# Two late tables of modulation weights loaded earlier, and a different schedule of modulation work in the second layer

## The chip, the cores and the metric

The kernel runs on one core of one Trainium2 chip. The metric is the device time of one execution in microseconds (us); the times given are those of several executions, and one more execution was taken with the hardware profiler. TensorE (PE, with its weight loads PEld) does the matmuls, VectorE (DVE), ScalarE (ACT) and GpSimd (POOL) the rest, and SyncE's queue (SP) issues nearly all transfers.

## What is computed

Two layers of a streaming encoder over 256 positions of width 2048, all in float32. Per layer:

```python
mod = (c_act @ w_mod[l] + b_mod[l]).reshape(bn, 6, d)     # c_act: one vector of 2048
shift_m, scale_m, gate_m, shift_f, scale_f, gate_f = ...  # six vectors of 2048
h = layer_norm(x) * (1.0 + scale_m) + shift_m
proj = h @ w_in[l]
uv, q_c, kv_c, k_r, sb, sc, sh, ag = jnp.split(proj, IN_SPLITS, axis=-1)
y_a = gmlp_mixer(uv, ...)            # u * (W_s LN(v) + b): groups U and V of the kernel
y_b = mla_mixer(q_c, kv_c, k_r, ...) # attention: group B
y_c = short_conv_mixer(sb, sc, sh, ...)   # groups E (sb) and C (sc, sh)
y_d = conformer_conv(ag, ...)        # a * sigmoid(g), a convolution over 31 positions: group D
y = jnp.concatenate([y_a, y_b, y_c, y_d], axis=-1) @ w_out[l]
x = layer_norm(ALPHA * x + (1.0 + gate_m) * y, post_mix_g[l], post_mix_b[l])
h = layer_norm(x) * (1.0 + scale_f) + shift_f
y = conv_ffn(h, ffn_w_up[l], ...)    # up to 2 x 5632 columns, gate convolution, down
x = layer_norm(ALPHA * x + (1.0 + gate_f) * y, post_ffn_g[l], post_ffn_b[l])
```

The six modulation vectors of a layer come from a product of one vector with a 2048 x 12288 matrix, 100 MB per layer. The kernel does this product on VectorE, while TensorE does the large products.

## The kernel before

**Large products.** Weights come in tiles of 1 MB (`raw_tile`, a ring of four buffers of 128 x 2048, which modulation weights, normalisation gains and a few others share). `weights` (L405 to L447) issues the load, lets ScalarE round each half tile to a `whi` (L442) and VectorE form the rest `wlo` (L443); each of these has a ring of four half tiles. The activations are split in the same way into the pairs `hT` (L459, L460), and TensorE adds up hi x hi, hi x lo and lo x hi (`mm`, L83). Some groups use the weights unsplit (`wexact`), with plain float32 matmuls. With `spare`, the first halves of a group go into buffers of another pool, the slots (eleven buffers of 128 x 1024, `thi` and `tlo`), which also hold the activations of the mixers and of the FFN.

**Order.** A group's units are run by `stream`: load a unit, then carry out what is pending (`flush`: the products of the unit before, the evacuation of a finished group), put this unit's products on the pending list, and then let `pump` take some modulation steps. The program text is then ordered by a scheduler that places instructions on each engine as their inputs come; on an engine they run strictly in that order.

**Modulation.** `mod_stream` is a generator that walks through the vectors in a fixed order. One step loads 1 MB of `w_mod` (L338) and multiplies and adds it on VectorE into `macc` (L246, the first of a vector L244). `RATES` says how many steps `pump` takes for each unit of a stage (`phase` sets the stage). `need` makes up for what is missing when a vector is used. A gate vector gets its bias in L345, is split (`mhi`, `mlo`) and spread over the partitions by TensorE into `ps_gate` (`gate_rows`). Layer 1's mixer gate is needed when the first 1024 columns of the output projection are done: there `done` calls `gate_of`, and `finish` (L675 to L679) scales and adds the columns.

**Layer 0's late columns.** Of layer 0's FFN shift and scale, only the first 1536 columns are ready when the FFN begins. The last 512 of each (`LATE_KT`) are computed during the first FFN units: eight loads of 1 MB (L315), four rows blocks of 128 each, with four VectorE instructions each. `first_group` multiplies the first gate columns with the three quarters of the input that are there, its `rest` follows with the last quarter after the units of two other groups.

**Start of a layer's products.** `first_group` (L510) loads its weights, normalises and transposes the input (`to_hT`: `xn` on ScalarE, `ps_xT` on TensorE, `hF` on ScalarE for the first 128 positions and on VectorE, L585, for the others), multiplies, and splits the input for the groups that follow. In layer 1 the first group is U, and `mix_u` (L851, a Gelu on ScalarE) evacuates it in the program's text before the next group, D, loads its weights. In layer 1's FFN `gated_first` (L1260) stands in the same way ahead of the next group's load.

Of the kernel before, what the change touches and what calls it, by code (L numbers as in the profile page):

```python
# [13 lines left out]
P = 128  # L14
D = 2048
# [10 lines left out]
C_UV, C_Q, C_SB, C_SC, C_AG = 0, 1024, 1728, 2240, 3264  # L26
# [5 lines left out]
SHIFT_M, SCALE_M, GATE_M, SHIFT_F, SCALE_F, GATE_F = range(6)  # L32
# [1 line left out]

RATES = [
    dict(B=1.3, C=1.6, out=2.1, first=1.2, up=0.68, down=0.83),
    dict(D=0.2, U=0.4, V=0, B=0.2, C=0.5, E=0.6, out=0.6, up=0.3, down=0.7),
]

STEPS = [  # L40
# [10 lines left out]
LATE_KT = 12  # L51
# [3 lines left out]
def encoder_kernel(ctx: ExitStack, tc: tile.TileContext, A: dict, consts: bass.AP, out: bass.AP):  # L55
    nc = tc.nc
# [13 lines left out]
    def raw_tile(name):  # L70
        return rawp.tile([P, 2048], F32, tag="raw", name=name)
# [16 lines left out]
    def slot(name, dtype=F32):  # L88
        return slotp.tile([P, 1024], dtype, tag="slot", name=name)
# [151 lines left out]
    def mod_step(acc, w, kt, first):  # L241
        col = cact[:, kt : kt + 1]
        if first:
            i = dve.tensor_scalar(out=acc, in0=w, scalar1=col, scalar2=None, op0=ALU.mult)  # L244
        else:
            i = dve.scalar_tensor_tensor(out=acc, in0=w, scalar=col, in1=acc, op0=ALU.mult, op1=ALU.add)  # L246
        held(i, "mod")
# [47 lines left out]
    def settle(i=0):  # L295
        l, m, acc, k0, k1 = late.pop(i)
        if m in (GATE_M, GATE_F):
            gate_rows(l, m, acc)
        elif (l, m) in ((1, SHIFT_F), (1, SCALE_F)):
            mod_rows(l, m, acc)  # L300
        else:
            mod_cols(l, m, k0, acc[:, k0 * P : k1 * P])

    def mod_stream(order):

        held_back = {}
        for l, m in order:
            if (l, m) == (0, GATE_F):  # L310

                for u in range(4):
                    for v, acc in held_back.items():
                        raw = raw_tile("wmod").rearrange("p (k c) -> p k c", k=4)
                        nc.sync.dma_start(  # L315
                            out=raw,
                            in_=A["w_mod"][0, 4 * u * P : 4 * (u + 1) * P, v * D + LATE_KT * P : (v + 1) * D].rearrange(
                                "(k p) c -> p k c", p=P
                            ),
                        )  # L320
                        for k in range(4):
                            mod_step(acc[:, LATE_KT * P :], raw[:, k, :], 4 * u + k, u + k == 0)
                        if u == 3:
                            late.append((0, v, acc, LATE_KT, KT))
                        yield
            while len(late) >= 2:
                if late[0][:2] in WITH_NORM:
                    yield
                else:
                    settle()  # L330
            acc = tmpp.tile([P, D], F32, tag="macc", name="macc", bufs=2)
            k1 = KT
            if l == 0 and m in (SHIFT_F, SCALE_F):
                held_back[m], k1 = acc, LATE_KT
            w = k1 * P
            for kt in range(KT):
                raw = raw_tile("wmod")
                nc.sync.dma_start(out=raw[:, :w], in_=A["w_mod"][l, kt * P : (kt + 1) * P, m * D : m * D + w])  # L338
                if kt == KT - 1 and m in (GATE_M, GATE_F):
                    row = raw_tile("brow")  # L340
                    nc.sync.dma_start(out=row[0:1, :], in_=A["b_mod"][l : l + 1, m * D : (m + 1) * D])
                mod_step(acc[:, :w], raw[:, :w], kt, kt == 0)
                if kt == KT - 1:
                    if m in (GATE_M, GATE_F):
                        dve.tensor_tensor(out=acc[0:1, :], in0=acc[0:1, :], in1=row[0:1, :], op=ALU.add)  # L345
                    late.append((l, m, acc, 0, k1))
                yield
                if kt == 1 and late and late[0][:2] not in WITH_NORM:
                    settle()

    mods = mod_stream(
        [(0, GATE_M), (0, SHIFT_F), (0, SCALE_F), (0, GATE_F), (1, SHIFT_F), (1, SCALE_F)]
        + [(1, SHIFT_M), (1, SCALE_M), (1, GATE_M), (1, GATE_F)]
# [3 lines left out]
    def phase(l, name):  # L357
        pace["rate"] = RATES[l][name]
# [16 lines left out]
    pending = []  # L375
# [22 lines left out]
    def held(i, kind):  # L398

        name, n = hold[kind]  # L400
        if n > 0:
            hold[kind][1] = n - 1
            tc.add_manual_dep(i.ins, name, order_dep, reason="the norm is what the next products wait for")
# [366 lines left out]
    def mixers(l, w_in, Y, hF=None, between=None):  # L770
# [77 lines left out]
        def mix_u(cps, _):  # L848
            Y["a"] = slot("ya").rearrange("p (j s) -> p j s", j=4)
            for b in range(2):  # L850
                act.activation(  # L851
                    out=Y["a"][:, 2 * b : 2 * b + 2, :],
                    in_=cps[b].rearrange("p (j s) -> p j s", j=2),
                    func=AF.Gelu_apprx_tanh,
                )
# [259 lines left out]
        if hF is not None:  # L1115
            return by_pieces(l, w_in, hF, between, mix_d, mix_u, mix_v, mix_b, mix_c, mix_e)
        phase(l, "U")
        mix_u(first_group(w_in, C_UV, f"U{l}", l, SHIFT_M, SCALE_M)[0], None)
        phase(l, "D")
        run(group(w_in, C_AG, 1024, f"D{l}", mix_d, spare=1))  # L1120
        phase(l, "V")
# [115 lines left out]
    def ffn_up(l, G):  # L1237
# [19 lines left out]
        def gated_first(cps, j0=0):  # L1257
            G.append(slot("g").rearrange("p (j s) -> p j s", j=4))
            for b in range(2):
                act.copy(G[j0 // 4][:, 2 * b : 2 * b + 2, :], cps[b].rearrange("p (j s) -> p j s", j=2))  # L1260
            for j in range(4):
                background.append(lambda j=j0 + j: gate_conv(j))

        cps, rest = first_group(w, 0, f"g{l}0", l, SHIFT_F, SCALE_F, LATE_KT // 4 if l == 0 else 4)
        if l == 0:

            gv = group(w, D_FF, 512, "v00", valued_pairs, nk=4, spare=1)
            gg = group(w, 512, 512, "g01", lambda cps, _: gated_first(cps, 4), nk=4)
            phase(l, "first")

            def late():
                needs(l, SHIFT_F, SCALE_F)()
                rest()
                gated_first(cps)

            for g, u in ((gv, 0), (gg, 0), (gv, 1), (gg, 1), (gv, 2), (gg, 2)):
                stream(lambda: g[1](u), lambda item, g=g, u=u: g[2](item, u))
            pending.append(late)
            phase(l, "up")
            for g, u in ((gv, 3), (gg, 3)):  # L1280
                stream(lambda: g[1](u), lambda item, g=g, u=u: g[2](item, u), STEPS[l]["up"])
            pending.extend([gv[3], gg[3]])
        else:
            gated_first(cps)

        for c0 in range(0, D_FF, 512):
            gi, j0 = c0 // 512, c0 // P
# [86 lines left out]
    def needs(l, *ms, k1=KT):  # L1374
        def before():
            for m in ms:
                need(l, m, k1)

        return before
# [114 lines left out]
```

## Time and profile before

| What | us |
|---|---|
| timed executions | 2326.01, 2333.79, 2332.75 (median 2332.75) |
| profiled execution | 2328.31 |
| its span, first to last instruction | 2326.5 |
| TensorE busy | 2255.9 |
| VectorE busy | 1792.9 |
| ScalarE busy | 1011.3 |
| mean granted TensorE clock | 0.986 |

Times within the span, from the timeline of TensorE: layer 0's FFN begins at 437, layer 1's U at 1218, its D at 1254, its output projection at 1467, its FFN at 1570. "Busy" is the sum of instruction times; matmuls are pipelined. The granted clock is the share of full speed that TensorE was allowed in a stretch.

### The profile page before, as it was taken

What the parts mean: (1) busy time and instruction counts of PE and PEld (TensorE: products, weight loads), DVE (VectorE), ACT (ScalarE), POOL (GpSimd) and SP (SyncE); (2) the same over time, 40 slices, a digit from 0 to 9 for tenths busy, and PEclk for the clock granted to TensorE, in tenths of its full rate; (3) what the DMA queues carried; (4) which work ended last, traced back from release to release, by engine and by line L of the source; (5) the groups of instructions that cost most, each with busy time, mean ns of one, the idle gap of its engine ahead of it and who ended that gap; (6) DMA issues with size and microseconds to landing.
All of it is one profiled execution on the core that took longest, in us unless ns stands there. A gap on an engine that the chain in (4) does not pass through costs nothing. (4 is left out here: it accounts for less than half of the span.)

```text
span 2326.5 us, 31205 instructions
## 1 busy us (share of the span) xinstructions
PE 2255.9 (97%) x12331; PEld 1936.7 (83%) x12331; DVE 1792.9 (77%) x2261; ACT 1011.3 (43%) x1443; POOL 37.6 (2%) x64
## 2 busy tenths in 40 slices
PE   6899999999999999999999999989999999999998
PEld 5688886698888888887889999869888888888786
DVE  6868997678888888988975799787777655665676
ACT  2221241245455454543544434435454454454553
POOL 2000000000000000000000000000000000000000
PEclk9899999999999999999999999999999999999999
DMA  9999889588988898897864576775767655555554
GB/s 340 372 316 327 293 298 380 198 299 292 327 310 316 293 325 320 303 345 282 302 217 162 166 245 229 264 257 184 246 235 265 232 181 194 186 188 193 176 203 145
DMA packets 228730, 605.17 MB, mean 260 GB/s; under 512 B 14676, under 2 KB 27204, under 8 KB 210916
## 3 DMA queue, kind: packets, MB, share of 16 engines
q1 hardware_dynamic: 227800, 602.30, 73.7%
q8 instruction: 96, 1.57, 0.3%
q0 software_dynamic: 784, 0.90, 0.1%
q14 instruction: 50, 0.41, 0.0%
HBM read 601.05 MB, written 2.10 MB: 259 GB/s over the span
## 5 line engine op out<-in xcount | busy, mean ns | idle before, releaser
L443 DVE TENSOR_TENSOR wlo<-wraw,whi 128x1024 fp32r<-128x1024 f32 (+1 forms) x622 | 739.5, 1214 | 337.4 <-ACT whi L442 305.9
L442 ACT CAST whi<-wraw 128x1024 fp32r<-128x1024 f32 (+1 forms) x622 | 633.0, 1044 | 735.9 <-PE g_c L83 208.6
L83 PE MATMUL d<-whi,a 128*128 128x512 f32 x1344 | 390.9, 392 | 0.0
L246 DVE SCALAR_TENSOR_TENSOR macc<-wmod,cact,macc 128x2048 f32<-128x2048 f32 (+2 forms) x180 | 358.2, 1990 | 29.6 <-DMA wmod<-in_w_mod_dram 28.7
L83 PE MATMUL v_c<-hT,whi 128*128 128x512 f32 (+1 forms) x1456 | 358.7, 384 | 0.0
L83 PE MATMUL g_c<-hT,whi 128*128 128x512 f32 (+1 forms) x1344 | 327.7, 382 | 0.0
L83 PEld LDWEIGHTS d<-whi,a 128*128 128x128 f32 x1344 | 254.4, 190 | 52.8
L83 PEld LDWEIGHTS v_c<-hT,whi 128*128 128x128 f32 x1456 | 259.3, 189 | 43.5
L83 PEld LDWEIGHTS g_c<-hT,whi 128*128 128x128 f32 x1344 | 238.7, 189 | 39.0
L83 PE MATMUL d<-wlo,a 128*128 128x512 f32 x672 | 235.1, 392 | 4.1 <-DVE wlo L443 4.0
L83 PEld LDWEIGHTS v_c<-hT,wlo 128*128 128x128 f32 x1400 | 194.5, 190 | 13.7
L83 PE MATMUL v_c<-hT,wlo 128*128 128x256 f32 x1400 | 203.9, 282 | 0.0
L83 PEld LDWEIGHTS g_c<-hT,wlo 128*128 128x128 f32 x1280 | 178.2, 190 | 11.8
L83 PE MATMUL g_c<-hT,wlo 128*128 128x256 f32 x1280 | 187.7, 282 | 0.0
L83 PEld LDWEIGHTS d<-wlo,a 128*128 128x128 f32 x672 | 127.2, 189 | 33.0 <-DVE wlo L443 6.2
L459 ACT CAST a<-g 128x512 fp32r<-128x512 f32 x132 | 80.6, 618 | 74.5 <-PE d L83 73.3
L83 PE MATMUL o<-whi,a 128*128 128x512 f32 x352 | 100.6, 394 | 0.0
L797 DVE SCALAR_TENSOR_TENSOR convD<-gluD,pm,convD 128x255 f32<-128x255 f32 (+25 forms) x240 | 99.2, 459 | 0.6
L460 DVE TENSOR_TENSOR a<-g,a 128x512 fp32r<-128x512 f32 x132 | 88.0, 684 | 12.1 <-ACT a L459 12.1
L83 PE MATMUL D_c<-hT,whi 128*128 128x256 f32 x432 | 84.0, 296 | 2.8 <-ACT hT L459 1.8
L246 DVE SCALAR_TENSOR_TENSOR qacc<-wmod,cact,qacc 128x1024 f32<-128x1024 f32 (+1 forms) x75 | 80.2, 1070 | 2.7 <-DMA wmod<-in_w_mod_dram 0.6
L83 PEld LDWEIGHTS o<-whi,a 128*128 128x128 f32 x352 | 66.8, 190 | 14.1 <-ACT whi L442 0.3
(312 smaller groups left out, 2547.7 us busy)
## 6 DMA issues: line engine op xcount, KB each, us to landing
wraw<-in_ffn_w_up_dram SPq DMA_DIRECT2D x168, 1024.0 KB, 5.4
wmod<-in_w_mod_dram SPq DMA_DIRECT2D x136, 1024.0 KB, 6.2
wraw<-in_ffn_w_down_dram SPq DMA_DIRECT2D x88, 1024.0 KB, 5.3
wmod<-in_w_mod_dram SPq DMA_DIRECT2D x64, 512.0 KB, 8.8
wraw<-in_w_in_dram SPq DMA_DIRECT2D x30, 1024.0 KB, 5.6
wexact<-in_w_in_dram SPq DMA_DIRECT2D x52, 512.0 KB, 7.4
wmod<-in_w_mod_dram SPq DMA_DIRECT2D x32, 768.0 KB, 6.3
wraw<-in_w_out_dram SPq DMA_DIRECT2D x24, 1024.0 KB, 6.4
```

What stands on the lines that cost most here:

```text
L83: pe.matmul(o, lhsT, rhs, start=start, stop=stop, skip_group_check=True)
L246: i = dve.scalar_tensor_tensor(out=acc, in0=w, scalar=col, in1=acc, op0=ALU.mult, op1=ALU.add)
L442: act.copy(hi[:, :m], r)
L443: i = dve.tensor_tensor(out=lo[:, :m], in0=r, in1=hi[:, :m].bitcast(F32), op=ALU.subtract)
L459: act.copy(hi, src)
L460: dve.tensor_tensor(out=lo, in0=src, in1=hi.bitcast(F32), op=ALU.subtract)
L797: dve.scalar_tensor_tensor(out=yd[:, j, 30 - k :], in0=glu[:, j, : S - 30 + k], scalar=CW(k, j), in1=yd[:, j, 30 - k :], op0=ALU.mult, op1 ...
```

## The change

It has three parts. In layer 1 the rates of the mixer's stages change: D from 0.2 to 0.8, U from 0.4 to 0 (no unit of U goes through `stream`), B from 0.2 to 0.3, C from 0.5 to 0.6. In layer 1, `mix_u` and `gated_first` go on the pending list, so that the next group's weights are loaded and split in the program's text before the evacuation. In layer 0, the first of four loads for each of the two late vectors (2 MB in all) goes into four slots, issued behind `first_group`'s loads, instead of into the ring of raw tiles one at a time.

```diff
 RATES = [
     dict(B=1.3, C=1.6, out=2.1, first=1.2, up=0.68, down=0.83),
-    dict(D=0.2, U=0.4, V=0, B=0.2, C=0.5, E=0.6, out=0.6, up=0.3, down=0.7),
+    dict(D=0.8, U=0, V=0, B=0.3, C=0.6, E=0.6, out=0.6, up=0.3, down=0.7),
 ]
...
+    def late_part(u, v, k0, nk, dst):
+        nc.sync.dma_start(
+            out=dst.rearrange("p (k c) -> p k c", k=nk),
+            in_=A["w_mod"][0, (4 * u + k0) * P : (4 * u + k0 + nk) * P, v * D + LATE_KT * P : (v + 1) * D].rearrange(
+                "(k p) c -> p k c", p=P
+            ),
+        )
+        return [dst[:, k * 512 : (k + 1) * 512] for k in range(nk)]
+
+    late_first = {}
+
+    def load_late_first():
+        for v in (SHIFT_F, SCALE_F):
+            late_first[v] = late_part(0, v, 0, 2, slot("wlate")) + late_part(0, v, 2, 2, slot("wlate"))
...
                 for u in range(4):
                     for v, acc in held_back.items():
-                        raw = raw_tile("wmod").rearrange("p (k c) -> p k c", k=4)
-                        nc.sync.dma_start(
...
+                        ws = late_first[v] if u == 0 else late_part(u, v, 0, 4, raw_tile("wmod"))
                         for k in range(4):
-                            mod_step(acc[:, LATE_KT * P :], raw[:, k, :], 4 * u + k, u + k == 0)
+                            mod_step(acc[:, LATE_KT * P :], ws[k], 4 * u + k, u + k == 0)
...
         phase(l, "U")
-        mix_u(first_group(w_in, C_UV, f"U{l}", l, SHIFT_M, SCALE_M)[0], None)
+        ups = first_group(w_in, C_UV, f"U{l}", l, SHIFT_M, SCALE_M)[0]
+        pending.append(lambda: mix_u(ups, None))
         phase(l, "D")
...
             gg = group(w, 512, 512, "g01", lambda cps, _: gated_first(cps, 4), nk=4)
+            load_late_first()
             phase(l, "first")
...
         else:
-            gated_first(cps)
+            pending.append(lambda: gated_first(cps))
```

How the scheduler's order moves is shown at three places. Line numbers of the changed program are 9 to 11 higher from the late columns on (L442 becomes L451, L443 L452, L460 L469, L585 L594, L851 L860).

**ScalarE at layer 1's step from U to D.** Before (`thi` and `whi` are D's weights, `hT` the split input, `ya` the evacuation of U):

```order
L459 CAST hT<-hF_9169 128x2x256
L459 CAST hT<-hF_9170 128x2x256 x2
L442 CAST whi<-wraw 128x1024 x2
L851 ACT_TABLE_LOAD
L851 ACTIVATE ya<-U_c_9387 128x512
L851 ACTIVATE ya<-U_c_9388 128x512
L442 CAST thi<-wraw 128x1024
L442 CAST whi<-wraw 128x1024 x14
```

With the change:

```order
L86 ACTIVATE xn<-x_96,rs_d0r_9367 128x512 x4
L451 CAST thi<-wraw 128x1024
L468 CAST hT<-hF_9171 128x2x256 x2
L468 CAST hT<-hF_9172 128x2x256 x2
...
L451 CAST whi<-wraw 128x1024 x2
L860 ACT_TABLE_LOAD
L860 ACTIVATE ya<-U_c_9391 128x512
L860 ACTIVATE ya<-U_c_9392 128x512
L451 CAST whi<-wraw 128x1024 x14
```

The first half tile of D's weights (`thi`) has moved from behind the evacuation of U to ahead of the casts of the input.

**VectorE from layer 1's norm to the end of D.** With the change (before, the only L244 or L246 of this stretch stood behind `tlo`, ahead of the last fourteen `wlo`):

```order
L244 TENSOR_SCALAR macc<-wmod,cact 128x2048
L594 TENSOR_SCALAR hF_9171<-ps_xT,mod_1_0_9313,mod_0_0_9293 128x128 x4
L452 TENSOR_TENSOR tlo<-wraw,thi 128x1024
...
L246 SCALAR_TENSOR_TENSOR macc<-wmod,cact,macc 128x2048
L594 TENSOR_SCALAR hF_9173<-ps_xT,mod_1_0_9313,mod_0_0_9293 128x128 x4
...
L452 TENSOR_TENSOR wlo<-wraw,whi 128x1024 x2
L246 SCALAR_TENSOR_TENSOR macc<-wmod,cact,macc 128x2048
L452 TENSOR_TENSOR wlo<-wraw,whi 128x1024
L246 SCALAR_TENSOR_TENSOR macc<-wmod,cact,macc 128x2048
L452 TENSOR_TENSOR wlo<-wraw,whi 128x1024 x5
L246 SCALAR_TENSOR_TENSOR macc<-wmod,cact,macc 128x2048
L452 TENSOR_TENSOR wlo<-wraw,whi 128x1024 x2
L246 SCALAR_TENSOR_TENSOR macc<-wmod,cact,macc 128x2048
L452 TENSOR_TENSOR wlo<-wraw,whi 128x1024 x7
```

Five more modulation steps stand between the splits of this stretch, the first of them ahead of the evacuation of the transposes (L585 before).

**VectorE where layer 1's output projection finishes its first 1024 columns.** Before (`wlo` are the projection's weights, `mlo` the gate's split, `yg` begins the finish):

```order
L246 SCALAR_TENSOR_TENSOR macc<-wmod,cact,macc 128x2048
L443 TENSOR_TENSOR wlo<-wraw,whi 128x1024
L345 TENSOR_TENSOR macc<-macc,brow 1x2048
L244 TENSOR_SCALAR macc<-wmod,cact 128x2048
L460 TENSOR_TENSOR mlo<-macc,mhi 128x1024 x2
L675 TENSOR_TENSOR yg<-o_000_11813,gate_2_12118 128x512
L675 TENSOR_TENSOR yg<-o_001_11814,gate_2_12118 128x512
```

With the change, first in group E and then in the projection:

```order
L452 TENSOR_TENSOR wlo<-wraw,whi 128x1024 x3
L246 SCALAR_TENSOR_TENSOR macc<-wmod,cact,macc 128x2048
L452 TENSOR_TENSOR wlo<-wraw,whi 128x1024
L354 TENSOR_TENSOR macc<-macc,brow 1x2048
L452 TENSOR_TENSOR wlo<-wraw,whi 128x1024
...
L469 TENSOR_TENSOR mlo<-macc,mhi 128x1024
L452 TENSOR_TENSOR wlo<-wraw,whi 128x1024 x4
L246 SCALAR_TENSOR_TENSOR macc<-wmod,cact,macc 128x2048
L452 TENSOR_TENSOR wlo<-wraw,whi 128x1024 x3
L246 SCALAR_TENSOR_TENSOR macc<-wmod,cact,macc 128x2048
L452 TENSOR_TENSOR wlo<-wraw,whi 128x1024
L684 TENSOR_TENSOR yg<-o_000_11838,gate_2_11984 128x512
```

The gate's bias has moved into E, its split ahead of the last units of the first columns; between it and the finish there are now weights and two modulation steps, and behind the finish, as before, four `wlo` ahead of the next step.

More of the change, by code (lines that the diff above doesn't have):

```diff
@@ L313, in mod_stream @@
                     for v, acc in held_back.items():
-                        raw = raw_tile("wmod").rearrange("p (k c) -> p k c", k=4)
-                        nc.sync.dma_start(
[L316 to L320, printed above, removed]
+                        ws = late_first[v] if u == 0 else late_part(u, v, 0, 4, raw_tile("wmod"))
                         for k in range(4):
-                            mod_step(acc[:, LATE_KT * P :], raw[:, k, :], 4 * u + k, u + k == 0)
+                            mod_step(acc[:, LATE_KT * P :], ws[k], 4 * u + k, u + k == 0)
                         if u == 3:
```

## The prediction

> **What bounds the kernel now.** I read the page's first part, then TensorE's waits, then the stages by windows.
>
> ```profile
> PE 2255.9 (97%) x12331; PEld 1936.7 (83%) x12331; DVE 1792.9 (77%) x2261; ACT 1011.3 (43%) x1443; POOL 37.6 (2%) x64
> ```
> ```profile
> PE o L83 <- DVE wlo L443: 5.5, 1, 5.5
> ...
> PE D_c L83 <- ACT thi L442: 2.7, 1, 2.7
> ...
> PE ps_mod L83 <- DVE macc L246: 1.4, 1, 1.4
> ```
> TensorE is busy 2255.9 of 2326.5 us, and the change takes no matmul away. So only the 70.6 us of idle time can be won, and what a gap does to the speed behind it. Three waits of this list lie where the change works: 5.5 (layer 1's output projection), 2.7 (layer 1, U to D), 1.4 (layer 0, late columns). The windows by stage (columns: length, busy us of PE, PEld, DVE, ACT, POOL, granted clock, DMA share, GB/s) show what else is short there:
>
> ```profile
> 462.00:512.00 50.00, 46.77 (x350) 45.11 (x349) 38.86 (x47) 16.86 (x22) 0.00 (x0) 0.93 0.92 331
> 1253.00:1304.00 51.00, 50.21 (x394) 49.62 (x395) 20.32 (x18) 17.97 (x19) 0.00 (x0) 0.97 0.58 187
> 1325.00:1363.00 38.00, 36.63 (x304) 36.12 (x303) 37.93 (x73) 15.05 (x25) 2.77 (x5) 1.00 0.69 221
> 1363.00:1437.00 74.00, 73.90 (x526) 68.62 (x526) 66.33 (x123) 29.11 (x46) 1.09 (x1) 1.00 0.66 231
> 1437.00:1467.00 30.00, 29.46 (x223) 28.59 (x222) 24.33 (x35) 12.46 (x17) 0.70 (x1) 0.94 0.69 238
> 1603.00:2072.00 469.00, 469.00 (x2688) 412.69 (x2687) 311.79 (x401) 234.60 (x348) 0.00 (x0) 1.00 0.64 217
> ```
> Layer 1's D (1253 to 1304) has VectorE idle for 30 us and a DMA share of 0.58: there is room. V and B (to 1363) have VectorE full. Layer 1's FFN (1603 to 2072) has no idle TensorE: fewer modulation steps there win nothing.
>
> A gap costs more than itself, as windows of 3.41 us show:
>
> ```profile
> 497.63:501.04 3.41, 1.91 (x16) 1.74 (x15) 3.33 (x4) 0.22 (x2) 0.00 (x0) 1.00 1.00 369
> 501.04:504.45 3.41, 1.97 (x8) 1.57 (x8) 0.23 (x1) 2.88 (x7) 0.00 (x0) 0.50 1.05 384
> 504.45:507.87 3.42, 3.13 (x8) 2.54 (x9) 3.24 (x7) 2.33 (x5) 0.00 (x0) 0.50 0.91 349
> ...
> 1088.13:1091.54 3.41, 2.21 (x10) 1.50 (x8) 3.41 (x4) 2.24 (x4) 0.00 (x0) 1.00 0.00 0
> 1091.54:1094.96 3.42, 2.27 (x10) 1.86 (x11) 3.42 (x3) 0.90 (x1) 0.00 (x0) 1.00 0.75 230
> ...
> 1251.98:1255.40 3.42, 1.61 (x11) 1.41 (x12) 1.63 (x2) 1.71 (x3) 0.00 (x0) 1.00 0.50 202
> 1255.40:1258.81 3.41, 3.41 (x18) 3.41 (x18) 0.00 (x0) 0.00 (x0) 0.00 (x0) 0.50 0.85 274
> ...
> 1521.60:1525.00 3.40, 0.17 (x1) 0.17 (x2) 3.40 (x6) 0.25 (x1) 0.00 (x0) 0.51 0.01 2
> 1525.00:1528.44 3.44, 3.44 (x9) 2.67 (x10) 3.44 (x4) 0.00 (x0) 0.00 (x0) 0.50 0.33 85
> ```
> Where TensorE was busy 1.61 to 1.97 us of such a window, the next one runs at a clock of 0.50; where it was 2.21, the next keeps 1.00. A full window at half clock loses 1.7 us of work.
>
> **The change part by part.** *U to D in layer 1.* ScalarE loads the Gelu table, evacuates U and only then rounds D's first weights (thi), for which TensorE waits:
>
> ```profile
> 1251.68 1.08 ACT L851 ACTIVATE ya<-U_c 128x512 f32<-128x512 f32 x2
> 1252.65 1.05 ACT L442 CAST thi<-wraw 128x1024 fp32r<-128x1024 f32 x1
> ```
> ```profile
> 1253.75 1.22 PE L83 MATMUL D_c<-hT,thi 128*128 128x256 f32 x8 [2.68 <-ACT thi L442]
> ```
> U's last product starts before 1253.75 - 2.68 = 1251.1, so the wait is all of table load, evacuation and rounding. Now thi stands ahead of the hT casts on ScalarE, and the table load and the evacuation behind the casts of D's next weights. Late next would be the splits of hT that D reads; VectorE has the last one done 2.9 before 1251.1:
>
> ```profile
> 1247.46 0.69 DVE L460 TENSOR_TENSOR hT<-hF,hT 128x512 fp32r<-128x512 f32 x1
> ```
> I take the whole gap, 2.7 (ScalarE's new order leaves nothing of it), and the half-clock window behind it, 1.7: **-4.4** (bounds 2.7 and 4.4).
>
> [...]
>
> *Modulation steps in D.* By VectorE's order six steps now run between layer 1's norm and D's end, where there was one. A step costs 2.35 (first row below), so five add 11.8 to 20.3 busy of 51. Nothing on TensorE waits if splits keep their lead:
>
> ```profile
> 1093.69 2.35 DVE L246 SCALAR_TENSOR_TENSOR macc<-wmod,cact,macc 128x2048 f32<-128x2048 f32 x1
> ```
> ```profile
> 1231.93 1.37 DVE L585 TENSOR_SCALAR hF<-ps_xT,mod,mod 128x128 f32<-128x128 f32 x4 [4.34 <-PE ps_xT L574]
> ...
> 1266.93 1.23 DVE L443 TENSOR_TENSOR wlo<-wraw,whi 128x1024 fp32r<-128x1024 f32 x1 [3.08 <-ACT whi L442]
> ...
> 1272.64 1.23 DVE L443 TENSOR_TENSOR wlo<-wraw,whi 128x1024 fp32r<-128x1024 f32 x1 [3.09 <-ACT whi L442]
> ```
> ```profile
> wmod<-in_w_mod_dram SPq DMA_DIRECT2D x136, 1024.0 KB, 6.2
> ```
> VectorE idles 3.1 in every unit of 5.7 us (1272.64 - 1266.93), more than a step. Each wmod goes through SP's queue and a raw tile between the weights: 5 MB more in the 51 us of the row is 103 GB/s, so about 290 with its 187; layer 0's 462 to 512 carried 331. The first step stands ahead of L585, which starts at 1231.9 after 4.34 idle. Its load takes the place of the weights that SP issued at 1223.7 in the row below; 1223.7 + 6.2 + 1.3 = 1231.2, 0.7 before VectorE gets to it. The later ones are requested when a step or a unit's splits release a tile; where one lands late, the split queued behind it still has the 3.1 of idle time as slack. **0**; without that cover each step can cost up to its landing, 6.2, less 3.1.
>
> ```profile
> 1223.70 25.97 SPq L428 DMA_DIRECT2D wraw<-in_w_in_dram  x3
> ```
>
> *The gate of layer 1's output projection.* Before, the end of the gate's sums, its split and the first chunk's finish run in one burst, and the next chunk's splits stand behind it:
>
> ```profile
> 1509.79 2.27 DVE L345 TENSOR_TENSOR macc<-macc,brow 1x2048 f32<-1x2048 f32 x1
> ...
> 1516.38 1.29 DVE L675 TENSOR_TENSOR yg<-o,gate 128x512 f32<-128x512 f32 x2 [0.76 <-ACT gate L86]
> ...
> 1523.57 4.61 DVE L443 TENSOR_TENSOR wlo<-wraw,whi 128x1024 fp32r<-128x1024 f32 x4
> ```
> ```profile
> 1524.83 0.79 PE L83 MATMUL o<-wlo,a 128*128 128x512 f32 x1 [5.53 <-DVE wlo L443]
> ```
> Six steps ahead means that the bias (L345) falls into E and the split among the first chunk's weights, so only the finish (1516.38 to 1523.57, 7.2) is left. The nearest row is layer 0's down projection, whose gate is ready early: finish, one modulation step (2.35), then the splits.
>
> ```profile
> 1092.69 0.50 PE L83 MATMUL d<-wlo,a 128*128 128x512 f32 x1 [2.35 <-DVE wlo L443]
> ```
> Here no step stands between, so nothing of the 2.35 should stay; I leave 0.1. Won: 5.5 - 0.1, and 1.8 of half clock (1524.83 to 1528.44): **-7.2** (bounds 4.9, if 2.35 stays, and 7.3).
>
> *Layer 0's late columns.* Their first 2 MB go into slots right behind the last of FFN's exact weights on SP's queue (first row), at 429.75 + 5.52 = 435.3. The slots' old readers are matmuls of the projection that ends there, so SP has nothing to wait for, and what it issues next, weights for the second value unit, waits for a gains tile anyway. VectorE's order now has three steps on them ahead of the first evacuation L585: by the median landing 435.3 + 8.8 = 444.1, before the 448.69 of that evacuation, so nothing is held up.
>
> ```profile
> 429.75 5.52 SPq L420 DMA_DIRECT2D wexact<-in_ffn_w_up_dram  x4
> ...
> wmod<-in_w_mod_dram SPq DMA_DIRECT2D x64, 512.0 KB, 8.8
> ...
> 448.69 1.37 DVE L585 TENSOR_SCALAR hF<-ps_xT,mod,mod 128x128 f32<-128x128 f32 x4
> ```
> In before, TensorE reaches the late shift and scale ahead of their sums:
>
> ```profile
> 496.73 3.11 DVE L246 SCALAR_TENSOR_TENSOR macc<-wmod,cact,macc 128x512 f32<-128x512 f32 x4
> ```
> ```profile
> 499.89 1.05 PE L83 MATMUL ps_mod<-onesR,macc 128*128 128x1 f32 x8 [1.40 <-DVE macc L246]
> 502.14 1.97 PE L574 MATMUL ps_xT<-cst,xn 128*128 128x128 f32 x8 [1.20 <-ACT xn L86]
> ```
> TensorE asks at 499.89 - 1.40 = 498.5, the last sum ends at 496.73 + 3.11 = 499.84. The stretch 462 to 512 is bound by transfers (share 0.92), and 2 MB fewer in it at 331 GB/s are 6 us; a quarter of that brings the sums ahead of TensorE. So the 1.4 goes. The chain ps_mod, xn, ps_xT, hF stays (1.2 before the transposes, and what follows). Of two half-clock windows one should stay, for the first window still holds that chain; the other's loss (3.13 / 2 = 1.6, of which I count 1.3 because the chain may end in it) goes: **-2.7** (0 to 4.1).
>
> *Given back.* The order has one more step in layer 1's C and the bias (2.3) in E, where VectorE is busy 66.3 of 74 and 24.3 of 30. I charge **+1.0** (0 to 6: both in full, 4.6, and most of a half-clock window). The evacuation moved behind the load in layer 1's FFN is worth 0: from 1603 on no gap stands in the row above.
>
> Sum: -4.4 + 0 - 7.2 - 2.7 + 1.0 = -13.3. The profiled execution took 2328.31 (span 2326.5 and 1.8 around it), so 2315.0. The three timed runs are 2326.01, 2333.79 and 2332.75: the median stands 4.4 above the profiled one, the mean of all four (2330.2) 1.9 above. I forecast **2317**.
>
> **The rivals.** *Given back in full* (17%): B's row has VectorE at 37.93 of 38, and everything pushed behind it waits; all 6 instead of 1: 2322. Against it: D ends 4.4 earlier for the convolution's taps too. *Only U to D counts* (15%): in layer 1's projection the finish alone still starves the splits, with a fresh half-clock window, and in layer 0 the chain behind ps_mod sets the time anyway; 4.4 - 1.0 won: 2327. For it speaks the 2.35 that stays in layer 0's down projection. *The steps starve D* (5%), the slower side: VectorE takes its work in order, so a step whose 1 MB has not landed holds the split behind it. If each of five waits 6.2, less the 3.1 of slack, and each gap costs a half-clock window, that is 5 x (3.1 + 1.7) = 24, net +10.7: 2341. It decides once landing exceeds the slack at every step; 462 to 512 speaks against it, where steps run 1.2 to a unit (rate 1.2) and none of TensorE's waits is for a split. *Gaps alone* (5%): the half-clock windows of U to D and of layer 0 come back at other gaps, so 2.7 + 7.2 + 1.4 - 1.0 = 10.3 is won: 2320. The profile shows half clock only behind little work, and U to D has none left. [...] *More* (3%): E's half clock (0.94 in its row) goes too, 1.7, with all upper bounds (17.5): 2313.
>
> **How the numbers follow.** The forecast has 55%, its own range 2311 to 2323. The range that leaves out no more than two in ten reaches to the second rival and its scatter: 2307 to 2331. A measurement of this kernel tells 0.3%, 7 us, from no change. Faster by more: nearly all of the forecast (52%), half of the first rival (8%), gaps alone and more (8%), 2% of the rest: 70%. Slower by more: 6%. Within: 24%.
>
> **What would show it.** Right: no wait of D_c for thi and clock 1.00 there; o's wait under 0.5; ps_mod not waiting for macc; D's step waits not followed by TensorE waits. Wrong: new waits of B_c, C_c or E_c for wlo over 2 us, clock 0.50 in new places, or g_c waiting for L585 at 447 because a wlate piece landed late.

## The result and the profile after

| | before | changed |
|---|---|---|
| timed executions, us | 2332.75 median (2326.01 to 2333.80, 5 runs) | 2317.16 median (2315.82 to 2321.52, 5 runs) |
| ratio to before | 1 | 0.9946, 95% interval 0.9934 to 0.9958 |
| profiled execution and its span, us | 2328.31, 2326.5 | 2317.50, 2315.7 |

The change makes the kernel 12.6 us faster by the ratio (9.8 to 15.4). The forecast was 2317. That the total fits so well is partly luck: of its three gains one came as forecast, one a fifth smaller, one hardly at all, and the loss that was charged did not come.

The first part of the page of the changed kernel:

```profile
PE 2249.8 (97%) x12331; PEld 1932.6 (83%) x12331; DVE 1791.8 (77%) x2261; ACT 1011.6 (44%) x1443; POOL 37.6 (2%) x64
```

TensorE carries the same 12331 products; its idle time went from 70.6 to 65.9 us (2315.7 - 2249.8), and its busy time fell by 6.1 as well. A product at half clock counts as busy for longer (one of `d`'s products of 128x512 takes 0.39 us as a rule and up to 0.78), and the half-clock windows that went at U to D and at o make up 3.6 of it by the forecast's way of counting (1.8 each). TensorE's waits, as far as they lie where the change works or beside it (line numbers behind 300 are 9 to 11 higher than before):

```profile
PE d L83 <- DVE wlo L452: 3.4, 2, 2.4
...
PE o L83 <- DVE wlo L452: 1.4, 1, 1.4
PE B_c L83 <- DVE wlo L452: 1.1, 1, 1.1
...
PE g_c L83 <- ACT hF L86: 0.6, 1, 0.6
...
PE ps_rD L83 <- DVE dgD L846: 0.3, 1, 0.3
```

The wait of D_c for thi (2.7) and that of ps_mod for macc (1.4) are in the list no more, and o waits 1.4 in place of 5.5. The stages by windows (length, busy us of PE, PEld, DVE, ACT, POOL, granted clock, DMA share, GB/s):

```profile
460.00:510.00 50.00, 48.08 (x369) 46.27 (x369) 40.03 (x52) 18.29 (x25) 0.00 (x0) 0.93 0.83 291
1252.00:1303.00 51.00, 51.00 (x399) 49.73 (x398) 29.38 (x27) 21.95 (x24) 0.00 (x0) 1.00 0.68 235
1358.00:1432.00 74.00, 73.83 (x511) 68.70 (x512) 70.71 (x128) 28.30 (x46) 1.10 (x1) 0.98 0.70 245
1432.00:1462.00 30.00, 29.75 (x235) 28.90 (x234) 26.67 (x38) 16.56 (x23) 0.70 (x1) 1.00 0.72 273
```

D has no idle TensorE left (51.00 of 51), a clock of 1.00 for 0.97, 9 us more of VectorE's work and 48 GB/s more of transfers. In C, VectorE is busier (70.7 of 74) and the clock a little lower; in E the clock went up from 0.94 to 1.00. In layer 0's first FFN groups the transfers fell from 331 to 291 GB/s, and the clock stayed at 0.93.

To see where time is won, the same product of TensorE (the same number in the order of the products into one tile) is looked up in two timelines. How much its start has moved against before, and how this grows or shrinks over a stage, gives this table, in us; minus is won. The columns "order", "rates" and "late" are experiments with one part of the change each, and "again" is a second profiled execution of the changed kernel.

| stage | forecast | changed | again | order | rates | late |
|---|---|---|---|---|---|---|
| start to layer 0's first FFN groups (untouched) | 0 | +1.9 | +3.5 | +9.1 | +3.1 | +1.4 |
| layer 0's late columns | -2.7 | -0.6 | -0.8 | +2.6 | -0.1 | -0.7 |
| rest of layer 0, norm (untouched) | 0 | -2.6 | -2.9 | -3.7 | -0.4 | -2.1 |
| layer 1, U to D | -4.4 | -4.7 | -4.8 | -4.8 | 0.0 | 0.0 |
| D, V and B | 0 | 0.0 | 0.0 | 0.0 | 0.0 | 0.0 |
| C and E | +1.0 | -0.4 | -0.9 | 0.0 | -0.4 | -0.2 |
| output projection | -7.2 | -5.8 | -5.8 | +1.3 | -5.9 | +0.2 |
| norm and first FFN group (untouched) | 0 | +1.0 | +1.5 | +0.4 | +2.2 | -0.1 |
| sum, with 0.0 to 0.1 in the FFN | -13.3 | -11.2 | -10.1 | +5.0 | -1.5 | -1.4 |

Two things stand out. In the stages where the change wins, the numbers repeat from execution to execution, to 0.1 in two of them (U to D: -4.7, -4.8, -4.8; output projection: -5.8, -5.8, -5.9) and to 0.2 in the late columns (-0.6, -0.8, -0.7). In C and E they do so only to 0.5 (-0.4, -0.9, -0.4), and where the change doesn't work, an execution differs from that of before by up to 9 us; the last section says what lies behind this. So a single profiled execution's total tells little here, its stages much.

### The profile page after: what moved, and what is told of

Read it like the earlier page. It is cut to its first block, busy times and chain, and to the rows that moved or that the text cites. A ratio compares the mean times of both kernels' runs of the same rounds, so it can differ in the third digit from the quotient of the medians.

```text
span 2315.7 us, 31206 instructions
## 1 busy us (share of the span) xinstructions
PE 2249.8 (97%) x12331; PEld 1932.6 (83%) x12331; DVE 1791.8 (77%) x2261; ACT 1011.6 (44%) x1443; POOL 37.6 (2%) x64
## 5 line engine op out<-in xcount | busy, mean ns | idle before, releaser
L452 DVE TENSOR_TENSOR wlo<-wraw,whi 128x1024 fp32r<-128x1024 f32 (+1 forms) x622 | 739.6, 1214 | 333.6 <-ACT whi L451 291.7
L451 ACT CAST whi<-wraw 128x1024 fp32r<-128x1024 f32 (+1 forms) x622 | 633.3, 1044 | 727.5 <-PE g_c L83 211.6
L246 DVE SCALAR_TENSOR_TENSOR macc<-wmod,cact,macc 128x2048 f32<-128x2048 f32 (+2 forms) x174 | 353.5, 2034 | 43.5 <-DMA wmod<-in_w_mod_dram 42.6
L806 DVE SCALAR_TENSOR_TENSOR convD<-gluD,pm,convD 128x255 f32<-128x255 f32 (+24 forms) x240 | 99.6, 461 | 0.5
L469 DVE TENSOR_TENSOR a<-g,a 128x512 fp32r<-128x512 f32 x132 | 88.2, 686 | 10.4 <-ACT a L468 10.3
L246 DVE SCALAR_TENSOR_TENSOR qacc<-wmod,cact,qacc 128x1024 f32<-128x1024 f32 (+1 forms) x75 | 80.3, 1070 | 2.6 <-DMA wmod<-in_w_mod_dram 0.5
L83 PEld LDWEIGHTS o<-whi,a 128*128 128x128 f32 x352 | 65.9, 188 | 14.2 <-ACT whi L451 0.6
```

Source lines behind the costliest of these rows:

```text
L83: pe.matmul(o, lhsT, rhs, start=start, stop=stop, skip_group_check=True)
L451: act.copy(hi[:, :m], r)
L452: i = dve.tensor_tensor(out=lo[:, :m], in0=r, in1=hi[:, :m].bitcast(F32), op=ALU.subtract)
L469: dve.tensor_tensor(out=lo, in0=src, in1=hi.bitcast(F32), op=ALU.subtract)
L806: dve.scalar_tensor_tensor(out=yd[:, j, 30 - k :], in0=glu[:, j, : S - 30 + k], scalar=CW(k, j), in1=yd[:, j, 30 - k :], op0=ALU.mult, op1 ...
```

## The experiments

**One part at a time.** The first takes only the new order of layer 1's evacuations:

```diff
-        mix_u(first_group(w_in, C_UV, f"U{l}", l, SHIFT_M, SCALE_M)[0], None)
+        ups = first_group(w_in, C_UV, f"U{l}", l, SHIFT_M, SCALE_M)[0]
+        pending.append(lambda: mix_u(ups, None))
...
-            gated_first(cps)
+            pending.append(lambda: gated_first(cps))
```

> The kernel before with one part of the change: the evacuation of layer 1's first groups (U, and the first gate group of its FFN) moves behind the load of the next weights; rates and layer 0 stay. The forecast's term for U to D: the 2.68 us wait of D_c for thi goes, and so does the half-clock window behind it (1.7): 4.4 less than before (bounds 2.7 and 4.4), and the 5.5 us wait of layer 1's o for wlo stays as it was. Rival, gaps alone: only 2.7 less, the half clock shows up at another place in D. Rival, the wait only changes its name: D_c waits for hT or wlo in its place and the time is within 1 us of before.

Measured: 2325.41 median (2320.96 to 2333.27, 12 runs) beside 2331.68 of before, ratio 0.9978 (0.9964 to 0.9991), that is 5.1 less (2.1 to 8.4). Its trace has -4.8 at U to D, and o's wait as before:

```profile
PE o L83 <- DVE wlo L443: 5.5, 1, 5.5
```

So U to D is a gain of its own, by the forecast's term with both its halves, wait and clock. The profiled execution happened to be a long one (2333.27), with 9.1 lost ahead of layer 0's late columns, where the kernels don't differ.

The second takes only the rates:

```diff
-    dict(D=0.2, U=0.4, V=0, B=0.2, C=0.5, E=0.6, out=0.6, up=0.3, down=0.7),
+    dict(D=0.8, U=0, V=0, B=0.3, C=0.6, E=0.6, out=0.6, up=0.3, down=0.7),
```

> The kernel before with the new rates of layer 1's modulation steps alone: U to D keeps its 2.7 us wait for thi and its half-clock window. The forecast's terms: the gate of the output projection -7.2 (its trace of the changed kernel says about -6: a wait of 1.4 instead of 5.5 and 1.8 of half clock), steps in D 0, given back in C and E +1.0: 6.2 less than before by the forecast, 5 to 6.5 by that trace. Rival, given back in full: only 1 to 2 less, with new waits of C_c or E_c for wlo. Rival, the steps starve D: more time than before, with D_c waiting for wlo behind steps whose loads are late.

Measured: 2325.60 median (2317.42 to 2330.41, 12 runs), ratio 0.9968 (0.9954 to 0.9983), 7.5 less (4.0 to 10.7). Its waits:

```profile
PE D_c L83 <- ACT thi L442: 2.7, 1, 2.7
...
PE o L83 <- DVE wlo L443: 1.4, 1, 1.4
```

The gate's gain needs the rates and nothing else; the two gains don't lean on each other. C and E give nothing back (-0.4), so the rival that gives back in full falls.

The third takes only the early load:

```diff
+            load_late_first()
...
-                        raw = raw_tile("wmod").rearrange("p (k c) -> p k c", k=4)
...
+                        ws = late_first[v] if u == 0 else late_part(u, v, 0, 4, raw_tile("wmod"))
```

> The kernel before with the early load of layer 0's first 2 MB of late shift and scale alone. The forecast's term: 2.7 less than before (bounds 0 and 4.1), because the sums are ready when TensorE asks and one of two half-clock windows goes. What the trace of the changed kernel suggests in its place: the 1.4 wait of ps_mod goes, but the chain ps_mod, xn, ps_xT, hF and both half-clock windows stay, so 0 to 1 less. Either way layer 1 is untouched: D_c's wait for thi 2.7 and o's for wlo 5.5.

Measured: 2328.46 median (2326.82 to 2341.14, 12 runs), ratio 0.9995 (0.9981 to 1.0009): no change that could be told. The interval (4.4 less to 2.1 more) would still hold the forecast's 2.7; the trace doesn't: it has -0.7 at the late columns and nothing of the change elsewhere. By their ratios the three parts sum to 13.8, beside the 12.6 of the whole.

**Are steps in D free?** Twice the rate there:

```diff
-    dict(D=0.8, U=0, V=0, B=0.3, C=0.6, E=0.6, out=0.6, up=0.3, down=0.7),
+    dict(D=1.6, U=0, V=0, B=0.3, C=0.6, E=0.6, out=0.6, up=0.3, down=0.7),
```

> The changed kernel with layer 1's rate in D at 1.6 in place of 0.8: about seven more modulation steps between its norm and the end of D. The forecast holds that steps in D cost nothing, VectorE idling 3.1 us in every unit of 5.7: within 1.5 us of the changed kernel (15.6 less than before by the medians), and no new wait of D_c; less of C's and E's work on VectorE could even win 1. Rival, the steps starve D: two steps in a unit take 4.7 of the 3.1 idle and each 1 MB load that is late holds the splits behind it; if half of the seven do so by 3.1 plus a half-clock window of 1.7, the time is 10 to 20 above the changed kernel, with D_c waiting for wlo.

Measured: 2317.52 median (2315.35 to 2323.12, 6 runs), ratio 0.9945 (0.9928 to 0.9961), not to be told from the changed kernel. TensorE's waits from U to the end of B:

```profile
PE B_c L83 <- DVE wlo L452: 1.6, 1, 1.6
PE V_t L83 <- DVE wlo L452: 0.5, 1, 0.5
```

D_c waits for nothing, though VectorE had up to two steps in a unit there. The rival of the starved splits in D falls at twice the dose. What the further steps cost in this trace comes right behind D: V's first products start 0.7 later, and B loses another 0.7. How near it was is seen in the changed kernel's VectorE timeline, where one step sits 4.83 us ahead of a split, waiting for its load:

```profile
1256.32 2.35 DVE L246 SCALAR_TENSOR_TENSOR macc<-wmod,cact,macc 128x2048 f32<-128x2048 f32 x1 [4.83 <-DMA wmod<-in_w_mod_dram]
1258.59 1.22 DVE L452 TENSOR_TENSOR wlo<-wraw,whi 128x1024 fp32r<-128x1024 f32 x1
...
1277.65 2.35 DVE L246 SCALAR_TENSOR_TENSOR macc<-wmod,cact,macc 128x2048 f32<-128x2048 f32 x1 [2.64 <-DMA wmod<-in_w_mod_dram]
```

That is more than the 3.1 of idle time that I had called the slack, and still cost nothing: the splits of D's first units had run ahead of TensorE, and the held split (1258.59) is one for the unit that begins at 1261.0. How far that lead goes was not measured.

**Why the late columns gave so little.** In the changed kernel, xn of the last quarter is made to wait for both column vectors. This takes that dependency away, for this quarter alone:

```diff
-        for m in (m_shift, m_scale):
+        for m in (m_shift, m_scale) if not (l == 0 and m_shift == SHIFT_F and k0 == LATE_KT) else ():
```

> The changed kernel, in which the normalized activations xn of layer 0's last quarter no longer wait for the late shift and scale columns. Theory: with the sums on time, the chain ps_mod, xn, ps_xT, hF sets the time there; xn (1.5 us on ScalarE) and a part of the transposes leave the chain, so the 1.2 us wait of ps_xT goes, and the window before it fills above the 2.1 us of work that brought half clock: 1.2 to 2.9 less than the changed kernel. Rival: TensorE is late there for the hF evacuation anyway (0.6 wait of g_c), the gap only moves from ps_xT to g_c and both half-clock windows stay: within 0.5 us.

Measured: 2317.18 median (2311.32 to 2321.90, 6 runs), ratio 0.9942 (0.9926 to 0.9958); the changed kernel beside it 2317.89. By the medians this can't be told from nothing; its trace can tell. The same stage there is -3.2 against before, where the changed kernel has -0.6 and -0.8: 2.4 to 2.6 more, in the upper half of what the theory expected. TensorE's timeline at this place, first of the changed kernel, then of this one:

```profile
500.45 1.05 PE L83 MATMUL ps_mod<-onesR,macc 128*128 128x1 f32 x8
502.70 1.82 PE L583 MATMUL ps_xT<-cst,xn 128*128 128x128 f32 x8 [1.20 <-ACT xn L86]
505.14 3.75 PE L83 MATMUL g_c<-hF,wexact 128*128 128x256 f32 x8 [0.62 <-ACT hF L86]
```
```profile
503.48 0.44 PE L583 MATMUL ps_xT<-cst,xn 128*128 128x128 f32 x2
503.75 0.95 PE L83 MATMUL ps_mod<-onesR,macc 128*128 128x1 f32 x8
504.57 1.15 PE L583 MATMUL ps_xT<-cst,xn 128*128 128x128 f32 x6
506.34 2.77 PE L83 MATMUL g_c<-hF,wexact 128*128 128x256 f32 x6 [0.62 <-ACT hF L86]
```

The chain set the time at this place, not the sums; with xn off the chain the 1.20 wait is gone and one of two half-clock windows too. (The four traces of kernels with this edit, this one and three below, have one half-clock window here; the eight without it have two or three.) At other places this execution lost what it had won here (3.1 at the start, more half clock in layer 0's down projection), all untouched by the edit.

**What is left of o's wait.** No modulation step on the last unit of a chunk and on the first of the next, at higher rates so that as many steps run:

```diff
-                stream(lambda: load(u), lambda item, u=u, unit=unit: unit(item, u), bg, not last)
+                stream(lambda: load(u), lambda item, u=u, unit=unit: unit(item, u), bg, not last and (name == "o0" or 0 < u < units - 1 or c0 + u == 0))
```

> The changed kernel without a modulation step on the last unit of an output or down projection's chunk and on the first unit of the next (rates raised, so that as many steps run in all; layer 0's output projection as it was). Theory of the prediction: the finish of 7.2 us alone does not starve the splits, the step beside it does. Then o's wait for wlo goes from 1.4 to about 0 and layer 0's d from 2.4 to about 0, with one or two half-clock windows (1.7 each) behind d: 4 to 7 less than the changed kernel. Rival, the burst alone starves the splits: o's 1.4 stays, as layer 1's d waits 1.0 with no step near it; 0 to 2 less.

Measured: 2315.08 median (2312.82 to 2316.98, 5 runs), ratio 0.9932 (0.9918 to 0.9946); 2.8 less than the changed kernel beside it by the medians, under the 4 to 7 that the theory gave. Its waits behind a projection's splits:

```profile
PE d L83 <- DVE wlo L452: 1.9, 3, 1.1
```

o waits for nothing any more, and the 2.4 of layer 0's d is gone (0.8 in two other pieces has come); the output projection takes 2.0 less than in the changed kernel and layer 0's d 2.5 less (1.9 against its second trace). So at these two places the finish alone doesn't starve the splits. In layer 1's down projection, where no modulation step stands near, d still waits 1.05, as it does in the changed kernel. There VectorE splits the gate (`mlo`) just ahead of the last split and the finish, and the finish follows without a wait for TensorE, so this work may be what makes it late; no run moved it:

```profile
2180.09 2.59 DVE L469 TENSOR_TENSOR mlo<-macc,mhi 128x1024 fp32r<-128x1024 f32 x2 [2.25 <-ACT mhi L468]
2182.60 1.22 DVE L452 TENSOR_TENSOR wlo<-wraw,whi 128x1024 fp32r<-128x1024 f32 x1
2183.73 1.28 DVE L684 TENSOR_TENSOR yg<-d,gate 128x512 f32<-128x512 f32 x2
```
```profile
2192.18 0.50 PE L83 MATMUL d<-wlo,a 128*128 128x512 f32 x1 [1.05 <-DVE wlo L452]
```

What the theory overrated is the half clock: layer 0's down projection has two half-clock windows here where the changed kernel has three, since those behind the column products (below) stay.

**Both edits**, and the changed kernel once more beside them:

> Both edits at once on the changed kernel: the sum of the two by the theories, 5 to 10 less than the changed kernel; by the rivals 0 to 2 less.

> The changed kernel once more, beside the other three. Both theories: 2317 us within its scatter. Its trace shows what is not of the change: if the windows in which the clock is halved lie on a grid of 3.41 us that stands elsewhere in every execution, then the same gaps of the first mixers and of layer 0's down projection cost another number of half-clock windows here than in the first trace, by up to 5 us, while U to D (no wait for thi) and o's wait of 1.4 are the same.

Measured: both edits 2313.04 (2311.48 to 2314.34, 4 runs), ratio 0.9923 (0.9909 to 0.9938); the changed kernel again 2317.89 (2313.12 to 2318.61, 5 runs), 0.9937 (0.9921 to 0.9952). Both edits win 4.9 by the medians, just under the 5 to 10 expected. The second trace of the changed kernel repeats the first at U to D and at o (1.4) and differs elsewhere, as expected.

**The column products and the clock.** TensorE's products of 128x1 turn a row of sums into columns. Layer 1's shift and scale get their columns by 32 such products each in layer 0's down projection. In every trace that has them, a window at half clock followed at both places, even though the window ahead counts as fully busy (before: 3.41 of 3.41 us ahead of the half clock at 1074.50 and at 1156.42). Here the two vectors take the way that the kernel has for others already (eight 4x512 products and small transposes), and layer 0's rate `down` goes from 0.92 to 1.0:

```diff
-    WITH_NORM = {(0, SHIFT_F), (0, SCALE_F), (1, SHIFT_M), (1, SCALE_M)}
+    WITH_NORM = {(0, SHIFT_F), (0, SCALE_F)}
...
-        elif (l, m) in ((1, SHIFT_F), (1, SCALE_F)):
+        elif l == 1:
             mod_rows(l, m, acc)
...
-            scalar=0.0 if m == SHIFT_F else 1.0,
+            scalar=0.0 if m in (SHIFT_F, SHIFT_M) else 1.0,
```

> The kernel with both edits, in which shift and scale of layer 1's mixers become columns as layer 0's projection already does it for other vectors: eight 4x512 products and four small transposes for each, in place of 32 column products of 128x1 (rate of layer 0's down projection 1.0 for 0.92, so that both are done before the norm). Theory: 32 products of 128x1 fill a 3.41 us window as busy, but the window behind it ran at 0.50 in every trace, so such products count for the clock as little as idle time; without them no half-clock window is left behind the two places in layer 0's down projection (near 1040 and 1140): 3.4 of half clock, and 2 x (3.7 - 2.1) of products, so 4 to 7 less than with both edits. Rival: the clock drops there for another reason (the transfers, the place), the half-clock windows stay behind the 4x512 products: 2 to 3 less; and the two splits on VectorE (1.2 each, twice) could hold d's splits and take that back.

> Both edits once more beside the run with rows: 2313 us within its scatter (2311 to 2315), with half-clock windows behind the 32 column products of 128x1 in layer 0's down projection.

Measured: with rows 2306.66 (2304.26 to 2311.84, 6 runs), ratio 0.9903 (0.9885 to 0.9921); both edits without rows, beside it, 2311.75 (2309.68 to 2313.40, 5 runs), 0.9918 (0.9902 to 0.9934). The windows of both edits at the two places:

```profile
1030.10:1033.50 3.40, 3.40 (x33) 3.40 (x32) 1.21 (x2) 0.44 (x1) 0.00 (x0) 1.00 0.98 369
1033.50:1036.90 3.40, 3.40 (x10) 2.80 (x10) 2.14 (x2) 2.06 (x3) 0.00 (x0) 0.50 0.79 323
1132.50:1135.90 3.40, 3.40 (x25) 3.14 (x25) 1.98 (x4) 1.61 (x4) 0.00 (x0) 1.00 0.73 246
1135.90:1139.30 3.40, 3.40 (x9) 2.64 (x8) 2.91 (x3) 0.86 (x1) 0.00 (x0) 0.50 0.58 235
```

With rows, the windows that hold the 4x512 products and transposes, and those behind them, run at 1.00:

```profile
1025.84:1029.25 3.41, 3.41 (x16) 2.06 (x15) 3.02 (x3) 1.24 (x2) 0.00 (x0) 1.00 0.66 267
1029.25:1032.66 3.41, 3.41 (x19) 2.55 (x18) 2.60 (x4) 2.31 (x4) 0.00 (x0) 1.00 0.92 305
1131.65:1135.06 3.41, 3.41 (x19) 1.92 (x17) 3.41 (x3) 2.50 (x4) 0.00 (x0) 1.00 0.66 271
1135.06:1138.48 3.42, 3.42 (x16) 2.84 (x16) 2.63 (x5) 2.38 (x5) 0.00 (x0) 1.00 0.86 302
```

At the two places themselves this execution wins 3.2 and 1.7 over both edits, 4.9 in all, in the range of the theory (4 to 7). Of the stage less is left. Up to the 900th product of layer 0's down projection it wins 7.3 against before, and both edits win 4.3 (3.4 in their other trace): 3.0 to 3.9 apart, at or above the rival's 2 to 3 and below the theory. Waits took some back: in this stretch d waits 3.9 for `wlo` and `whi`, where both edits wait 1.5. So the sizes alone don't decide against the rival; the windows at 1.00 behind the 4x512 products do. By the medians this version is 5.1 below both edits, with ratios whose intervals overlap. The rate of layer 0's down projection shifts with this edit, and with it the steps of later stages, so the total is not that of the columns alone, and it can't be said how much of the new waits is the rate's. This is the fastest version that was run, 25.6 below before by the medians.

## Why the prediction was right, point by point

*U to D: -4.4 forecast, -4.7 measured.* Right in mechanism and size. On ScalarE the table load and the evacuation now stand behind D's first weights, and TensorE is into D by 1249.5:

```profile
1249.08 1.28 ACT L860 ACT_TABLE_LOAD   x1
1250.37 1.09 ACT L860 ACTIVATE ya<-U_c 128x512 f32<-128x512 f32 x2
```
```profile
1249.52 0.48 PE L83 MATMUL D_c<-hT,thi 128*128 128x256 f32 x2
```

Before the first product of D 2.9 was won, behind it 1.8, which is the half-clock window. Had this gap cost no clock, 2.7 would have been won, the term's lower bound; the measurement decides against that.

*Steps in D: 0 forecast, 0.0 measured*, and no wait of D_c at twice the rate either, where V and B lost 0.7 each. Right, with more room in D than I had reckoned with.

*Gate of the output projection: -7.2 forecast, -5.8 measured.* The mechanism was right: the bias moved into E, the split among the first chunk's weights. The failed step is "no step stands between, so nothing of the 2.35 should stay; I leave 0.1": 1.4 stayed. A modulation step does stand there, ahead of the last split and so ahead of the finish. VectorE and then TensorE of the changed kernel:

```profile
1502.12 2.34 DVE L246 SCALAR_TENSOR_TENSOR macc<-wmod,cact,macc 128x2048 f32<-128x2048 f32 x1
1504.38 1.22 DVE L452 TENSOR_TENSOR wlo<-wraw,whi 128x1024 fp32r<-128x1024 f32 x1
1505.52 1.28 DVE L684 TENSOR_TENSOR yg<-o,gate 128x512 f32<-128x512 f32 x2
...
1512.70 4.61 DVE L452 TENSOR_TENSOR wlo<-wraw,whi 128x1024 fp32r<-128x1024 f32 x4
```
```profile
1513.96 0.50 PE L83 MATMUL o<-wlo,a 128*128 128x512 f32 x1 [1.42 <-DVE wlo L452]
```

In the experiment without that step, the finish waits for TensorE's sums and not the other way round:

```profile
1504.85 1.29 DVE L684 TENSOR_TENSOR yg<-o,gate 128x512 f32<-128x512 f32 x2 [0.18 <-PE o L83]
```

TensorE's products around it stand 1.1 later in that trace (o's 500th product), so that the finish of the changed kernel starts 1.8 late by comparison (1505.52 - 1504.85 + 1.1). I looked at what stands behind the finish and not at what stands ahead of it. Without the step the wait is gone, so the value of 0.1 belonged to another kernel, and of the signs named for a right forecast one failed: o's wait was to be under 0.5. The half clock (1.8) went as forecast: with a gap of 1.4, the window that holds most of it still has 2.4 us of products.

*Late columns: -2.7 forecast, -0.6 to -0.8 measured in four traces* (-0.4 with D at 1.6). This is the step that was wrong. The wait of ps_mod, 1.4, did go: the first product behind the chain starts 1.5 earlier against the stage's beginning. The failed step is "of two half-clock windows one should stay": both stayed, and the second is now full of work that runs at half clock, which takes 0.8 back:

```profile
499.77:503.18 3.41, 2.12 (x18) 1.89 (x17) 1.82 (x2) 1.77 (x4) 0.00 (x0) 1.00 0.99 348
503.18:506.59 3.41, 2.78 (x10) 1.92 (x9) 1.96 (x5) 3.33 (x8) 0.00 (x0) 0.50 1.02 418
506.59:510.01 3.42, 3.42 (x10) 2.70 (x9) 2.12 (x4) 0.32 (x1) 0.00 (x0) 0.50 0.79 295
```

I had the chain (ps_mod, xn, ps_xT, hF) as a thing that stays and priced only the wait ahead of it. But the chain has only a few small products in 6 us, and with it alone left (2.12 us busy in the window from 499.77) the next window still ran at 0.50; taking xn and its wait of 1.2 out of it won 2.4 to 2.6, taking away the 1.4 ahead of it 0.6 to 0.8.

*Given back in C and E: +1.0 forecast, -0.4 and -0.9 measured.* VectorE got busier in C and E (70.7 of 74, 26.7 of 30) and nobody waited for it. The half-clock window of E is gone in the first trace and one at 1359.9 has come; in the second trace it is at 1457.0. Neither was forecast, and the signs for a wrong forecast named clock 0.50 in new places; since the window stands elsewhere in two traces of the same kernel, which of them comes is not of the change alone.

*The sum.* -13.3 was forecast and -11.5 measured in the stages that the change touches; the two misses on the one side (1.4 and 2.1) were half made good by what was not given back (1.4) and by U to D (0.3). The allowance of 2.0 for the profiled execution of before being a fast one was on the low side: it stood 3.4 below the median of 29 later executions (2331.68).

*The rivals.* Given back in full, only U to D, and the steps starving D fell with the experiments on one part and on D. Gaps alone fell at U to D and at o, where the half-clock windows went and no others came for them there, and was true of the late columns, which is where I had not put it.

## What to carry over

Look up the same product in two traces and take the difference over a stage: the stages that this change won in repeat to 0.1 or 0.2 us here, while an untouched stage was up to 9.1 apart from one trace to another. When a wait is removed ahead of a chain of small steps, price the chain too: at the late columns the wait of 1.4 went, both half-clock windows behind it stayed, and 0.6 to 0.8 was won of the 2.7 forecast. And where a burst on VectorE starves the splits behind it (o waited 5.5 before, 1.4 with the change), look at what delays the burst's start as well as at what follows it.

## What the runs showed of the hardware that was not expected

**Busy is not busy to the clock.** I had read the half clock as following on a window with under 2 us of TensorE's busy time. The changed kernel has such a window behind one that counts as full:

```profile
1073.21:1076.62 3.41, 3.41 (x33) 3.41 (x32) 0.69 (x1) 0.46 (x1) 0.00 (x0) 1.00 1.05 413
1076.62:1080.03 3.41, 3.41 (x10) 2.79 (x10) 2.14 (x2) 2.06 (x3) 0.00 (x0) 0.50 0.15 63
```
```profile
1072.99 3.71 PE L83 MATMUL ps_mod<-onesR,macc 128*128 128x1 f32 x32
```

All of it is products with one column of moving data, 0.116 us each. Sixteen of them (2.0 us) in a window with 1.4 to 1.9 us of others (they overlap) were enough too, ahead of the half clock in E in the second trace of the changed kernel:

```profile
1453.68 0.61 PE L83 MATMUL ps_var<-onesR,sqD 128*128 128x1 f32 x4
...
1455.07 1.40 PE L83 MATMUL ps_var<-onesR,sqD 128*128 128x1 f32 x12
```

Leaving the 128x1 products out of the count, the windows at full clock that are quoted here and in the prediction hold at most 1.9 us of products where half clock follows (1.61 at U to D), and 2.21 where it doesn't. All windows of the twelve traces from 20 us on, laid out on the grid on which the half-clock windows of each trace stand, bear this out. Of 112 full-clock windows with under 1.4 us of other products, every one was followed by half clock; of 7583 with over 2.1, none; in between, it happened to some. With the 128x1 products counted as busy, 65 windows with over 2.1 us lost the clock. (In the traces of before and changed alone it is all of 16, none of 1263, 8 of 22 in between, and 11 with the 128x1 products counted.) A window that is at half clock itself needs more of them: behind 1.97 and 2.78 us the clock stayed at 0.50 (late columns, before and changed), behind 3.13 it came back. That replacing these products by wide ones removes the half clock was shown at two places; that the amount of moving data is what counts is an inference.

**The windows stand elsewhere in every execution.** The half-clock windows are 3.41 us long or twice or three times that, and their starts, counted from the first instruction, leave 2.72, 1.43, 2.92 and 1.33 when divided by 3.4133 in four executions (before, changed, changed again, order only). The 3.4133 is read from the traces: the full-clock stretch of 747.52 us from 1572.85 in before is 219 times that. The same gap thus falls across two windows in one execution and into one in another. Layer 0's d begins at 1092.69 in before after a wait of 2.35 for wlo; the two windows around it hold 2.21 and 2.27 us of products, and the clock stays at 1.00. In the changed kernel it begins at 1092.37 after 2.37; the window from 1090.28 holds 1.32, and the next one ran at 0.50. Up to the last product, half clock adds up to 58 us before, 58 and 51 in the two traces of the changed kernel and 68 with the new order alone, with the differences above all in layer 0's first stages, which are the same work in each of them. Where the windows stand is a cause of the differences between traces: the second trace of the changed kernel has a half-clock window at 241.8 that the first has not, and loses 1.7 there against it, in the same work. The 29 executions of before beside the first experiments lie between 2323.7 and 2338.1; how much of this scatter it explains was not measured. The sum of half clock alone doesn't tell: the second trace of the changed kernel has 7 us less of it and is 1.1 longer.
